# Two decoder layers on one core: the FFN up projection by Strassen's algorithm over pairs of chunks

## The chip, the core and the metric

The kernel runs on one core of a Trainium2 chip, as one program with one launch. The metric is its time on the device in microseconds (us), the median of several executions. The core has five engines that run their own queues in order and wait for each other through semaphores: TensorE (PE in the profile, its weight loads PEld), VectorE (DVE), ScalarE (ACT), GpSimd (POOL) and SyncE (SP), which issues the loads here.

## The reference, cut to what matters

Two layers over 256 tokens of width 1024. Each layer has two half-step FFNs of width 2816, a mixer of three attention branches between them, and a small gated embedding at its end.

```python
def swiglu(x, w1, w3, w2):
    return (jax.nn.silu(x @ w1) * (x @ w3)) @ w2

for i in range(DEPTH):                                   # DEPTH = 2
    h = h + 0.5 * swiglu(rms_norm(h, g_ffn1[i]), w1_a[i], w3_a[i], w2_a[i])
    u = rms_norm(h, g_mix[i])
    h = h + hybrid_mixer(u, ...)
    h = h + 0.5 * swiglu(rms_norm(h, g_ffn2[i]), w1_b[i], w3_b[i], w2_b[i])
    ple_gate = jax.nn.sigmoid(rms_norm(h, g_ple[i]) @ w_ple_gate[i])
    h = h + ple_gate * (p[i] @ w_ple_proj[i])
out = rms_norm(h, g_final)                               # x: (1, 256, 1024) float32
```

All inputs and the output are float32. So there are four FFNs; the change is in their up projections, `x @ w1` and `x @ w3`.

## The kernel before

**Three products for one.** Every float32 operand is split into a high part in a shorter format (`hi`, a ScalarE copy) and the rest (`lo`, a VectorE subtraction); `mm3` (L94 to L97) multiplies hi·hi, hi·lo and lo·hi into one PSUM bank. `load` (L76 to L87) fetches a weight tile of 128x1024 (0.5 MB) into `raw` (4 buffers), and splits it into `whi` and `wlo` (7 buffers each, shared by the whole program).

**An FFN.** The normalized, transposed input lies in `xhi`, `xlo` as 128 rows by 2 token blocks (`tb`) by 8 slices of the model width (`kt`) by 128 tokens; the row factor `r[tb]` of the norm is applied after the product. The width 2816 is cut into 11 chunks of 256 (`NFC`), and a chunk of `w13` holds 256 columns of `w1` and 256 of `w3`, so that one PSUM bank of 512 takes both. `up(c)` multiplies a chunk: 2 token blocks by 8 slices by 3 matmuls of 128x512, 48 in all, from four weight tiles. ScalarE then forms silu of one half (`act`, L203), VectorE the gated product (`pr`, L205). `turn(c)` transposes the product on TensorE and splits it (`fhi`, `flo`); `down` multiplies it by two tiles of `w2`, 24 matmuls, into four banks (`acc`) that gather over all chunks.

**What sets the order.** The loop over chunks writes `up(c)`, then `turn(c-1)`, then `down(c-2)`. A scheduler at build time reorders within the limits of dependences and buffers; at run time each engine takes its list in order, so an instruction that waits holds up all behind it on its engine. The program has eight PSUM banks: two for products (`mm`), two for transposes (`tr`), four for `acc`. GpSimd does the small arithmetic of the norms, on tiles of one column, and three adds of 128x512 in `start_r` (L800) at the program's beginning. `start` loads the input for the first FFN and its first chunk's weights; `soon` and `later` load the constants.

## Time and profile before

| what | value |
|---|---|
| median of 3 runs | 1354.6 us (1354.47 to 1354.67) |
| profiled execution: time, span | 1354.69 us, 1352.9 us |
| granted TensorE clock over the span | 0.997 |
| VectorE's weight splits (L86, 128x1024) | 420 of 1.22 us |
| ScalarE's weight copies (L85, 128x1024) | 420 of 1.05 us |
| weight loads of the four FFNs, 0.5 MB each | 260, 4.3 to 4.5 us from issue to landing |
| loads over the span | 174 GB/s |

How to read the rows below: a row of the timeline has the start in us, the duration (of all its instructions from the first's start to the last's end, where `x` is over 1), the engine, the line, the operation, its output and inputs by the program's names, and in brackets how long the engine had been idle and what ended that. A row of a group has the busy time and the mean of one in ns behind the bar. Durations of matmuls overlap: the distance of two starts is what one costs.

### The profile page before, as it was taken

What the parts mean: (1) busy time and instruction counts of PE and PEld (TensorE: products, weight loads), DVE (VectorE), ACT (ScalarE), POOL (GpSimd) and SP (SyncE); (2) the same over time, 40 slices, a digit from 0 to 9 for tenths busy, and PEclk for the clock granted to TensorE, in tenths of its full rate; (3) what the DMA queues carried; (4) which work ended last, traced back from release to release, by engine and by line L of the source; (5) the groups of instructions that cost most, each with busy time, mean ns of one, the idle gap of its engine ahead of it and who ended that gap; (6) DMA issues with size and microseconds to landing.
All of it is one profiled execution on the core that took longest, in us unless ns stands there. A gap on an engine that the chain in (4) does not pass through costs nothing.

```text
span 1352.9 us, 17897 instructions
## 1 busy us (share of the span) xinstructions
PE 1339.4 (99%) x6720; PEld 1118.3 (83%) x6720; DVE 815.5 (60%) x1190; ACT 731.6 (54%) x1122; POOL 49.3 (4%) x110
## 2 busy tenths in 40 slices
PE   8999999999999999999999999999999999999997
PEld 6888889979788888888888888898788788888886
DVE  6655566666658655555765555665667686655555
ACT  5544456665775544444654444566667745544445
POOL 2000000001000000000100000000010000000000
PEclk9999999999999999999999999999999999999999
DMA  7855547524337565555555555473435465555542
GB/s 261 278 187 190 187 130 223 172 98 152 125 125 218 164 203 187 189 189 190 162 187 187 187 187 187 141 224 126 141 109 160 156 204 173 184 191 187 190 160 83
DMA packets 68343, 236.61 MB, mean 175 GB/s; under 512 B 8225, under 2 KB 8865, under 8 KB 68257
## 3 DMA queue, kind: packets, MB, share of 16 engines
q1 hardware_dynamic: 67824, 234.43, 53.3%
q8 instruction: 52, 0.85, 0.3%
q10 hardware_dynamic: 432, 1.05, 0.2%
q14 instruction: 35, 0.28, 0.1%
HBM read 234.40 MB, written 1.05 MB: 174 GB/s over the span
## 4 chain that ended last, share of the span: by engine, by line
PE 97%; ACT 1%; POOL 1%; DMA 1%; DVE 0%; SPq 0%; issue 0%; POOLq 0%; ACTq 0%
PE mm L95 22%; PE mm L97 21%; PE mm L96 21%; PE acc L95 8%; PE acc L97 8%; PE acc L96 8%; PE tr L216 1%; PE tr L143 1%; PE acc L519 1%; PE tr L512 1%; PE acc L605 1%; PE acc L587 1%; PE tr L475 1%; PE acc L486 1%; DMA xraw<-in_xT 1%; PE acc L543 0%
## 5 line engine op out<-in xcount | busy, mean ns | idle before, releaser
L86 DVE TENSOR_TENSOR wlo<-raw,whi 128x1024 fp32r<-128x1024 f32 (+3 forms) x450 | 535.4, 1201 | 274.7 <-ACT whi L85 255.7
L85 ACT CAST whi<-raw 128x1024 fp32r<-128x1024 f32 (+3 forms) x450 | 456.0, 1028 | 262.0 <-PE acc L97 135.0
L95 PE MATMUL mm<-whi,xhi 128*128 128x512 f32 (+1 forms) x1032 | 404.3, 392 | 1.8 <-ACT whi L85 1.8
L96 PE MATMUL mm<-wlo,xhi 128*128 128x512 f32 (+1 forms) x1032 | 402.1, 390 | 0.6 <-DVE wlo L86 0.6
L97 PE MATMUL mm<-whi,xlo 128*128 128x512 f32 (+1 forms) x1032 | 402.3, 390 | 0.0
L95 PEld LDWEIGHTS mm<-whi,xhi 128*128 128x128 f32 x1032 | 194.0, 188 | 43.2 <-ACT whi L85 2.5
L96 PEld LDWEIGHTS mm<-wlo,xhi 128*128 128x128 f32 x1032 | 194.4, 188 | 40.8 <-DVE wlo L86 2.2
L97 PEld LDWEIGHTS mm<-whi,xlo 128*128 128x128 f32 x1032 | 194.2, 188 | 40.9 <-DVE xlo L129 0.9
L95 PE MATMUL acc<-whi,fhi 128*128 128x512 f32 x352 | 141.0, 402 | 0.0
L203 ACT ACTIVATE act<-mm,r 128x256 f32<-128x256 f32 x88 | 41.8, 475 | 177.2 <-PE mm L97 177.2
L97 PE MATMUL acc<-whi,flo 128*128 128x512 f32 x352 | 137.2, 392 | 0.0
L96 PE MATMUL acc<-wlo,fhi 128*128 128x512 f32 x352 | 136.6, 390 | 0.0
L205 DVE SCALAR_TENSOR_TENSOR pr<-mm,r,act 128x256 f32<-128x256 f32 x88 | 42.3, 481 | 130.9 <-ACT act L203 130.9
L97 PEld LDWEIGHTS acc<-whi,flo 128*128 128x128 f32 x352 | 66.0, 188 | 14.7
L95 PEld LDWEIGHTS acc<-whi,fhi 128*128 128x128 f32 x352 | 66.2, 188 | 13.2 <-ACT fhi L128 1.1
L96 PEld LDWEIGHTS acc<-wlo,fhi 128*128 128x128 f32 x352 | 66.3, 188 | 12.7
L95 PE MATMUL mm<-xhi,whi 128*128 128x256 f32 x256 | 73.9, 288 | 0.0
L97 PE MATMUL mm<-xhi,wlo 128*128 128x256 f32 x256 | 72.4, 283 | 0.0
L96 PE MATMUL mm<-xlo,whi 128*128 128x256 f32 x256 | 72.4, 283 | 0.0
L95 PEld LDWEIGHTS mm<-xhi,whi 128*128 128x128 f32 x256 | 48.9, 191 | 2.0 <-issue 2.0
L96 PEld LDWEIGHTS mm<-xlo,whi 128*128 128x128 f32 x256 | 49.0, 191 | 0.0
L97 PEld LDWEIGHTS mm<-xhi,wlo 128*128 128x128 f32 x256 | 48.9, 191 | 0.0
(213 smaller groups left out, 1361.5 us busy)
## 6 DMA issues: line engine op xcount, KB each, us to landing
raw<-in_w13b SPq DMA_DIRECT2D x88, 512.0 KB, 4.4
raw<-in_w13a SPq DMA_DIRECT2D x84, 512.0 KB, 4.5
raw<-in_wg SPq DMA_DIRECT2D x48, 512.0 KB, 3.8
...
```

The lines of the kernel that those rows point to most:

```text
L85: A.copy(hi[:, c], raw[:, c])
L86: V.tensor_tensor(out=lo[:, c], in0=raw[:, c], in1=hi[:, c].bitcast(F32), op=ALU.subtract)
L95: PE.matmul(o, lhs[0], rhs[0], start=first, stop=False)
L96: PE.matmul(o, lhs[0], rhs[1], start=False, stop=False)
L97: PE.matmul(o, lhs[1], rhs[0], start=False, stop=last)
L143: PE.transpose(t[:, j * P : (j + 1) * P], h[tb][:, k * P : (k + 1) * P], ident)
L203: A.activation(act, o[:, :FC], AF.Silu, scale=r[tb])
L205: V.scalar_tensor_tensor(out=pr, in0=o[:, FC:], scalar=r[tb], in1=act, op0=ALU.mult, op1=ALU.mult)
L216: PE.transpose(t[:, j * S + tb * P : j * S + (tb + 1) * P], prs[tb][:, j * P : (j + 1) * P], ident)
L475: PE.transpose(t[:96, j * P : (j + 1) * P], f[:, 4 * u + j, :], ident)
L486: PE.matmul(o[:, P : 3 * P], q[:, P : 2 * P], k, start=True, stop=True)
L512: PE.transpose(t[:, j * P : (j + 1) * P], e[:, j * P : (j + 1) * P], ident)
```

## The change

Chunks 0 to 9 are taken in five pairs, chunk 10 is multiplied first, as before. For a pair the input (two token blocks by two halves of the model width) and the weights (two halves of the model width by two chunks) are each seen as two by two blocks, and Strassen's algorithm, in Winograd's form, makes the four blocks of the result from 7 products of sums of blocks in place of 8 plain ones.

- `x_forms`, once per FFN, scales the input by the norm's factor (`spread` lays `r` along the free axis) and forms the seven left operands. GpSimd adds `xhi` and `xlo` back together (4 adds of 128x512), VectorE multiplies and adds, and every form is split again. Four of them overwrite `xhi`, `xlo`.
- `w_forms`, once per pair, loads eight tiles (`wr`, 10 buffers; two halves `u` of each of the four blocks). GpSimd forms four differences of 128x1024 for each `u` (`sub`), three of them in place, one in `t2`. ScalarE and VectorE split 14 tiles (`split_w`) in place of 8.
- `pair` runs products 1, 6, 2, 5, 7, 3, 4 (12 matmuls each) into three banks, with the sums of the results in between: `m1` and `m5` are copied out by ScalarE, `u2`, `m5` and `m1` are summed by VectorE, one add by GpSimd. `turn` for the chunks before stands between products, and their `down` after the pair.

A pair has 84 up matmuls in place of 96. The first FFN loads chunk 10 first; the scratch memory of the DMA and two tiles of other stages are made smaller for room.

```diff
+    def split_w(w):
+        hi = wp.tile([P, U], F32R, tag="whi", name=nm("whi"), bufs=7)
+        lo = wp.tile([P, U], F32R, tag="wlo", name=nm("wlo"), bufs=7)
+        A.copy(hi, w)
+        V.tensor_tensor(out=lo, in0=w, in1=hi.bitcast(F32), op=ALU.subtract)
+        return hi, lo
...
+            def gated(c, tb, a, b, scale=None):
+                act = fp.tile([P, FC], F32, tag="act", name=nm("act"))
+                pr = fp.tile([P, FC], F32, tag="pr", name=nm("pr"), bufs=6)
+                if scale is None:
+                    A.activation(act, a, AF.Silu)
+                    V.tensor_tensor(out=pr, in0=b, in1=act, op=ALU.mult)
+                else:
+                    A.activation(act, a, AF.Silu, scale=scale)
+                    V.scalar_tensor_tensor(out=pr, in0=b, scalar=scale, in1=act, op0=ALU.mult, op1=ALU.mult)
+                prs[c, tb] = pr
+
...
+            def quarter(a, at=None):
+                if at is None:
+                    q = [fp.tile([P, 4, P], F32R, tag=f"q{i}", name=nm("q"), bufs=3) for i in range(2)]
+                else:
+                    tb, n = at
+                    q = [x[:, tb, 4 * n : 4 * n + 4, :] for x in (xhi, xlo)]
+                split_T(a.rearrange("p (j t) -> p j t", j=4), *q)
+                return q
+            def x_forms():
+                rbc = fp.tile([P, S], F32, tag="rbc", name=nm("rbc"), bufs=1)
+                spread(r, rbc)
+                a = {}
+                for tb in range(TB):
+                    for n in range(2):
+                        t = a[tb, n] = t512("xn")
+                        t4 = t.rearrange("p (j t) -> p j t", j=4)
+                        c = slice(4 * n, 4 * n + 4)
+                        G.tensor_tensor(
+                            out=t4, in0=xhi[:, tb, c, :].bitcast(F32), in1=xlo[:, tb, c, :].bitcast(F32), op=ALU.add
+                        )
+                        rb = rbc[:, None, tb * P : (tb + 1) * P].to_broadcast([P, 4, P])
+                        V.tensor_tensor(out=t4, in0=t4, in1=rb, op=ALU.mult)
+                s1, s2 = t512("s1"), t512("s2")
+                V.tensor_tensor(out=s1, in0=a[1, 0], in1=a[1, 1], op=ALU.add)
+                V.tensor_tensor(out=s2, in0=s1, in1=a[0, 0], op=ALU.subtract)
+                f = {1: quarter(a[0, 0]), 6: quarter(s2), 2: quarter(a[0, 1]), 5: quarter(s1, (0, 0))}
+                V.tensor_tensor(out=a[1, 0], in0=a[0, 0], in1=a[1, 0], op=ALU.subtract)
+                f[7] = quarter(a[1, 0], (0, 1))
+                V.tensor_tensor(out=s2, in0=a[0, 1], in1=s2, op=ALU.subtract)
+                f[3] = quarter(s2, (1, 0))
+                f[4] = quarter(a[1, 1], (1, 1))
+                return f
+            def w_forms(p):
+                f = {i: [None, None] for i in range(1, 8)}
+                ws = []
+                for u in range(2):
+                    w = {}
+                    for kh, nh in ((0, 0), (0, 1), (1, 1), (1, 0)):
+                        w[kh, nh] = fp.tile([P, U], F32, tag="wr", name=nm("wr"), bufs=10)
+                        nc.sync.dma_start(w[kh, nh], w13[li, 2 * p + nh, 2 * kh + u])
+                    ws.append(w)
+                def sub(out, a, b):
+                    G.tensor_tensor(out=out, in0=a, in1=b, op=ALU.subtract)
+                for u, w in enumerate(ws):
+                    f[1][u] = split_w(w[0, 0])
+                    sub(w[0, 0], w[0, 1], w[0, 0])
+                    t2 = fp.tile([P, U], F32, tag="t2", name=nm("t2"), bufs=2)
+                    sub(t2, w[1, 1], w[0, 0])
+                    f[6][u] = split_w(t2)
+                    f[2][u] = split_w(w[1, 0])
+                    sub(w[0, 1], w[1, 1], w[0, 1])
+                    sub(w[1, 0], w[1, 0], t2)
+                for i, q in ((5, (0, 0)), (7, (0, 1)), (3, (1, 1)), (4, (1, 0))):
+                    for u, w in enumerate(ws):
+                        f[i][u] = split_w(w[q])
+                return f
+            def product(o, x, w, start=False):
+                for kt in range(4):
+                    m = [y[:, (kt % 2) * 512 : (kt % 2) * 512 + 512] for y in w[kt // 2]]
+                    mm3(o, [y[:, kt, :] for y in x], m, start and kt == 0, kt == 3, skip_group_check=True)
+            def pair(p, fx, middle):
+                fw = w_forms(p)
+                oa, ob, oc = bank_mm(), bank_mm(), bank_tr()
+                product(oa, fx[1], fw[1], True)
+                m1 = t512("m1")
+                A.copy(m1, oa)
+                product(ob, fx[6], fw[6], True)
+                u2 = t512("u2")
+                V.tensor_tensor(out=u2, in0=ob, in1=m1, op=ALU.add)
+                product(oa, fx[2], fw[2])
+                gated(2 * p, 0, oa[:, :FC], oa[:, FC:])
+                middle()
+                product(oc, fx[5], fw[5], True)
+                m5 = t512("m5")
+                A.copy(m5, oc)
+                G.tensor_tensor(out=m5, in0=m5, in1=m1, op=ALU.add)
+                product(ob, fx[7], fw[7])
+                V.tensor_tensor(out=m5, in0=ob, in1=m5, op=ALU.add)
+                gated(2 * p + 1, 1, m5[:, :FC], m5[:, FC:])
+                product(oc, fx[3], fw[3])
+                V.tensor_tensor(out=u2, in0=oc, in1=u2, op=ALU.add)
+                gated(2 * p + 1, 0, u2[:, :FC], u2[:, FC:])
+                product(ob, fx[4], fw[4])
+                V.tensor_tensor(out=m1, in0=ob, in1=m1, op=ALU.add)
+                gated(2 * p, 1, m1[:, :FC], m1[:, FC:])
...
-            prs = {}
-            for c in range(NFC):
-                prs[c] = up(c)
-                if first and c == 1:
-                    soon()
-                if first and c == 3:
+                        mm3(acc[2 * tb + n], f, w, c == last and j == 0, c == last - 1 and j == 1)
+
+            up(last)
+            if first:
+                soon()
+            fx = x_forms()
+            acc.extend(bank_acc() for _ in range(4))
+            done = [last]
+            for p in range(NP):
+                def middle(cs=tuple(done)):
+                    for c in cs:
+                        turn(c)
+
+                pair(p, fx, middle)
+                if first and p == 0:
                     later()
-                if c == 5 and aside is not None:
+                if p == 2 and aside is not None:
                     aside()
-                if c == 1:
-                    acc.extend(bank_acc() for _ in range(4))
-                if c >= 1:
-                    turn(c - 1, prs[c - 1])
-                if c >= 2:
-                    un = load2([c - 2])
+                for c in done:
+                    un = load2([c])
                     for tb in range(TB):
                         for n in range(2):
-                            down([c - 2], un, tb, n)
-            turn(NFC - 1, prs[NFC - 1])
-            cs = [NFC - 2, NFC - 1]
-            un = load2(cs)
+                            down([c], un, tb, n)
+                done = [2 * p + 1, 2 * p]
+            for c in done:
+                turn(c)
+            un = load2(done[::-1])
             ro = []
             for tb in range(TB):
                 for n in range(2):
-                    down(cs, un, tb, n)
+                    down(done[::-1], un, tb, n)
...
-            un.append(load(a["w13a"][0, 0, k // 2], step=512))
+            un.append(load(a["w13a"][0, NFC - 1, k // 2], step=512))
```

**VectorE, from the second pair to the third of the first FFN.** In the rows, `wlo<-raw` is a split of a `w2` tile (or, before, of any weight), `wlo<-wr` and `wlo<-t2` a split of a weight form, `pr` a gated product, `flo` a split of transposed products; the numbers behind the names tell buffers apart. Before, a chunk's rows were these:

```order
L86 TENSOR_TENSOR wlo_220_1089<-raw_218_1087,whi_219_1088 128x1024
L129 TENSOR_TENSOR flo_156_767<-tr_190_953,fhi_155_766 128x512
L86 TENSOR_TENSOR wlo_223_1095<-raw_221_1093,whi_222_1094 128x1024
L86 TENSOR_TENSOR wlo_226_1125<-raw_224_1123,whi_225_1124 128x1024
L205 SCALAR_TENSOR_TENSOR pr_213_1049<-mm_211_1022,r_29_203,act_212_1047 128x256
L86 TENSOR_TENSOR wlo_229_1131<-raw_227_1129,whi_228_1130 128x1024
```

Now the end of one pair (`u2`, `m1` of the second) and the beginning of the next are these; the split behind `m1` is that of the next pair's first form:

```order
L327 TENSOR_TENSOR u2_158_666<-tr_156_639,u2_158_666 128x512
L87 TENSOR_TENSOR wlo_185_812<-raw_183_810,whi_184_811 128x1024
L215 TENSOR_TENSOR pr_171_748<-u2_158_666,act_170_747 128x256
L330 TENSOR_TENSOR m1_157_652<-mm_155_638,m1_157_652 128x512
L94 TENSOR_TENSOR wlo_195_857<-wr_186_840,whi_194_856 128x1024
L215 TENSOR_TENSOR pr_173_765<-m1_157_652,act_172_764 128x256
L94 TENSOR_TENSOR wlo_198_864<-t2_196_861,whi_197_863 128x1024
L94 TENSOR_TENSOR wlo_200_868<-wr_189_846,whi_199_867 128x1024
L94 TENSOR_TENSOR wlo_202_874<-wr_190_848,whi_201_873 128x1024
L94 TENSOR_TENSOR wlo_205_881<-t2_203_878,whi_204_880 128x1024
L94 TENSOR_TENSOR wlo_207_885<-wr_193_854,whi_206_884 128x1024
```

The six splits are those of forms 1, 6 and 2 of the first half and then of the second. They go on with forms 5, 7 and 3, and the add of product 6 into `u2` stands behind them:

```order
L94 TENSOR_TENSOR wlo_209_891<-wr_186_840,whi_208_890 128x1024
L94 TENSOR_TENSOR wlo_211_895<-wr_190_848,whi_210_894 128x1024
L94 TENSOR_TENSOR wlo_213_899<-wr_187_842,whi_212_898 128x1024
L94 TENSOR_TENSOR wlo_215_903<-wr_191_850,whi_214_902 128x1024
L94 TENSOR_TENSOR wlo_217_907<-wr_188_844,whi_216_906 128x1024
L315 TENSOR_TENSOR u2_228_951<-mm_225_923,m1_227_937 128x512
```

**GpSimd in the same place.** Before, its list had only the norm's factors here, from the beginning of the first FFN to its end:

```order
L124 TENSOR_TENSOR r_29_203<-ms_28_201,mhalf_80 128x1
L124 TENSOR_TENSOR r_31_207<-ms_30_205,mhalf_80 128x1
L164 TENSOR_SCALAR ss1_321_1566<-ss_318_1561 128x1
L166 TENSOR_SCALAR ms_322_1568<-ss_318_1561,ss1_321_1566 128x1
L168 TENSOR_TENSOR r_323_1570<-ms_322_1568,mhalf_80 128x1
```

Now the add of the second pair and the eight differences of the third stand there:

```order
L322 TENSOR_TENSOR m5_167_714<-m5_167_714,m1_157_652 128x512
L285 TENSOR_TENSOR wr_186_840<-wr_187_842,wr_186_840 128x1024
L285 TENSOR_TENSOR t2_196_861<-wr_188_844,wr_186_840 128x1024
L285 TENSOR_TENSOR wr_187_842<-wr_188_844,wr_187_842 128x1024
L285 TENSOR_TENSOR wr_189_846<-wr_189_846,t2_196_861 128x1024
L285 TENSOR_TENSOR wr_190_848<-wr_191_850,wr_190_848 128x1024
L285 TENSOR_TENSOR t2_203_878<-wr_192_852,wr_190_848 128x1024
L285 TENSOR_TENSOR wr_191_850<-wr_192_852,wr_191_850 128x1024
L285 TENSOR_TENSOR wr_193_854<-wr_193_854,t2_203_878 128x1024
```

The first difference overwrites `wr_186`, which the first split of the pair reads (the fifth row of the second piece).

**TensorE, from product 2 of the second pair on.** `mm_154` is the bank of products 1 and 2, `mm_155` that of 6, 7 and 4, `tr_156` that of 5 and 3:

```order
L105 MATMUL mm_154_637<-whi_136_599,q_50_278 128x512
L103 MATMUL mm_155_638<-whi_142_613,xhi_68 128x512
L104 MATMUL mm_155_638<-wlo_143_614,xhi_68 128x512
L103 MATMUL tr_156_639<-whi_138_605,xhi_68 128x512
L104 MATMUL tr_156_639<-wlo_139_606,xhi_68 128x512
```

The first two matmuls of product 7 were moved ahead of product 5. They write into the bank of product 6, which the first add into `u2` reads.

55 lines of the change are left out of this document (29 added, 26 removed).

## The prediction

> **What bounds the kernel now.** I read the page first (busy time, chain of work that ended last), then the timeline of one stage, then the few places where GpSimd does real work, because that is the engine which the change loads.
>
> ```profile
> PE 1339.4 (99%) x6720; PEld 1118.3 (83%) x6720; DVE 815.5 (60%) x1190; ACT 731.6 (54%) x1122; POOL 49.3 (4%) x110
> ...
> PE 97%; ACT 1%; POOL 1%; DMA 1%; DVE 0%; SPq 0%; issue 0%; POOLq 0%; ACTq 0%
> ```
>
> TensorE is busy for 99% of the span and holds 97% of the chain; GpSimd is nearly empty. So fewer matmuls would pay directly, as long as nothing else becomes late. What a matmul is worth is read from the timeline of an FFN:
>
> ```profile
> 40.13 0.39 PE L97 MATMUL mm<-whi,xlo 128*128 128x512 f32 x1
> ...
> 44.89 0.39 PE L97 MATMUL mm<-whi,xlo 128*128 128x512 f32 x1
> ...
> 45.12 0.60 PE L216 MATMUL tr<-ident,pr 128*128 128x128 f32 x4
> ...
> 45.48 0.48 PE L95 MATMUL acc<-whi,fhi 128*128 128x512 f32 x1
> ```
> ```profile
> 61.74 8.29 SPq L84 DMA_DIRECT2D raw<-in_w13a  x4
> ...
> 145.78 8.29 SPq L84 DMA_DIRECT2D raw<-in_w13a  x4
> ```
>
> Between the first two rows lie 21 matmuls, so one costs (44.89 − 40.13) / 21 = 0.227 us from start to start (its 0.39 us overlap the next). Four transposes take 0.36. The last two rows are the first weight loads of chunks five apart: a chunk lasts 84.04 / 5 = 16.81 us, which is 72 matmuls and the transposes; two chunks 33.6. TensorE has no gap there.
>
> **What goes.** A pair needs 84 up matmuls in place of 96: 12 × 0.227 = 2.7 us, and 20 pairs give 54.4 us. That is all that can be won; TensorE's own work for a pair becomes 132 × 0.227 + 0.8 = 30.7 us.
>
> **What comes, and its prices.** Per pair 8 subtractions of 128x1024 on GpSimd, 14 weight splits (ScalarE copy, VectorE subtract) in place of 8, four VectorE adds of 128x512, one GpSimd add of 128x512. The prices:
>
> ```profile
> L86 DVE TENSOR_TENSOR wlo<-raw,whi 128x1024 fp32r<-128x1024 f32 x420 | 508.7, 1223 | 258.4 <-ACT whi L85 243.7
> ...
> L205 DVE SCALAR_TENSOR_TENSOR pr<-mm,r,act 128x256 f32<-128x256 f32 x88 | 42.3, 481 | 130.9 <-ACT act L203 130.9
> L129 DVE TENSOR_TENSOR flo<-tr,fhi 128x512 fp32r<-128x512 f32 x44 | 30.1, 684 | 0.1
> ```
> ```profile
> 53.17 2.36 DVE L86 TENSOR_TENSOR wlo<-raw,whi 128x1024 fp32r<-128x1024 f32 x2 [0.68 <-ACT whi L85]
> ```
> ```profile
> 17.20 1.28 DVE L86 TENSOR_TENSOR wlo<-raw,whi 128x512 fp32r<-128x512 f32 x2
> ```
> ```profile
> L85 ACT CAST whi<-raw 128x1024 fp32r<-128x1024 f32 x420 | 434.6, 1049 | 255.4 <-PE acc L97 133.4 <-PE mm L97 85.1 <-PE mm L96 25.2
> ```
> ```profile
> L161 POOL TENSOR_TENSOR ss<-ss 128x1 f32<-128x1 f32 x1 | 0.2, 193 | 6.4 <-ACT junk L157 6.4
> ```
>
> A split costs VectorE 1.22 us alone and 2.36 − 1.22 = 1.14 in a row; a 128x512 operation 0.68 and 1.28 − 0.69 = 0.59; a gate product 0.48; a copy costs ScalarE 1.05. GpSimd has three 128x512 adds, and they show more than a price:
>
> ```profile
> 8.93 0.69 DVE L86 TENSOR_TENSOR wlo<-raw,whi 128x512 fp32r<-128x512 f32 x1
> ...
> 9.44 1.34 POOL L800 TENSOR_TENSOR xsq<-xsq,xsq 128x512 f32<-128x512 f32 x1 [8.48 <-ACT xsq L791]
> 9.90 1.43 DVE L86 TENSOR_TENSOR wlo<-raw,whi 128x512 fp32r<-128x512 f32 x1 [0.28 <-ACT whi L85]
> ...
> 13.06 0.69 DVE L793 TENSOR_TENSOR xsq<-xraw 128x512 f32<-128x512 f32 x1
> 13.11 1.80 POOL L800 TENSOR_TENSOR xsq<-xsq,xsq 128x512 f32<-128x512 f32 x1 [2.33 <-ACT xsq L791]
> ...
> 13.66 1.78 DVE L86 TENSOR_TENSOR wlo<-raw,whi 128x512 fp32r<-128x512 f32 x1
> ```
> ```profile
> 14.98 1.62 POOL L800 TENSOR_TENSOR xsq<-xsq,xsq 128x512 f32<-128x512 f32 x1
> 15.37 1.50 DVE L134 SCALAR_TENSOR_TENSOR xlo<-xraw,gcol,xhi 128x256 fp32r<-128x256 f32 x1
> ...
> 16.65 1.05 PE L804 MATMUL acc<-ones,xsq 128*128 128x1 f32 x8 [0.18 <-POOL xsq L800]
> ```
>
> The VectorE split at 9.90 takes 1.43 us instead of 0.69 and ends at 11.33, 0.55 after GpSimd's add (9.44 + 1.34 = 10.78). The second add runs 1.80 us and ends at 14.91, 1.16 after VectorE's operation (13.75); the split from 13.66 ends at 15.44, 0.53 after that add; the third add ends at 16.60, again 1.16 after it; the last row ends at 16.87, 0.27 behind it. So in all these rows **a GpSimd operation and a VectorE operation with two SBUF inputs take turns**, without a gap, each waiting for the other's end; the split, with two SBUF inputs, is the commonest VectorE operation. Its turn takes 0.53 us for 512 columns, so 1.07 for 1024. GpSimd's turn takes 1.16 for 512. For 1024 no row exists: if all of 1.16 grows with the columns it is 2.32; if all of the 0.193 of a one-column add is fixed, 0.193 + 2 × 0.967 = 2.13. I take 2.2, near the middle, since the fixed part is small either way.
>
> The Trainium skill (GPSIMD Engine Reference, section 3.1) gives 4497 ns for a two-input fp32 add of 2048 columns on GpSimd against 2293 on VectorE and advises against elementwise work there. Half of it, an estimate of 2.25 us, would make the whole result some 7 us later than mine.
>
> **One pair in its steady state** (third to fifth of an FFN), from the end of product 4 of the pair before to the end of its own product 4. The order rows say what stands behind what. The first split of the new pair is queued on VectorE behind the add into `m1`, which waits for product 4; every subtraction of the pair waits for that split, because it overwrites the tile.
>
> - The `m1` add 0.69, the first split 1.14 and a gate product of 0.48: 2.3 us.
> - GpSimd then goes through six subtractions (four of the first half, two of the second) before the second `t2`; three splits take turns between them, since form 6 must wait for the first `t2` and the fourth subtraction for the split of `w[1, 0]`: 6 × 2.2 + 3 × 1.07 = 16.4.
> - Two more subtractions, seven splits and the add into `u2` that is queued behind them: 2 × 2.2 + 7 × 1.1 + 0.69 = 12.8. ScalarE's seven copies (7.3) and the `m1` copy run beside.
> - TensorE's first two matmuls of product 7 wait for that add (same PSUM bank), and all of product 5 stands behind them: products 7, 5, 3, 4 are still to come: 48 × 0.227 = 10.9.
>
> Sum 42.4, and ten handovers between engines at about 0.05 (the third add ends at 16.60, its reader starts at 16.65): **42.9 us against 33.6**. Down products, product 1, half of 6 and product 2 lie inside the first three items. TensorE's 30.7 us are no longer the bound; about 12 us of each pair it stands still.
>
> The second pair has its first split and two subtractions ahead of `m1`: 42.9 − 1.1 − 4.4 = about 37. The first pair begins with the up projection of chunk 10. From the last residual add before it to the first `u2` VectorE has 21 operations of 512 columns, 13 splits and 4 small ones (21 × 0.59 + 13 × 1.14 + 1.5 = 28.7), and GpSimd 7 subtractions and 4 adds (20.0), of which I let 17.5 stand in VectorE's way, the others falling beside operations that read PSUM; then 36 matmuls (8.2): 54.4. The tail is two rounds of down products of 10.9 and some 2.0 for transposes and their copies.
>
> An FFN: 54.4 + 37 + 3 × 42.9 + 23.8 = 243.9 us. Before: 11 × 16.81 + 1.1 = 186.0. Four times the difference is 232 us. In the first FFN the last piece of `xT` now stands on SP behind `ident` and `h`, 1.1 MB, some 3 us at the 341 GB/s below. The profiled run took 1354.69 us with a span of 1352.9 (median of the runs 1354.6, the same for this purpose): 1354.7 + 235 = **1590 us**. With the bounds of the subtraction, 37 on the path of each FFN: 148 × (−0.07 or +0.12) = −10 or +18.
>
> **Costed at nothing:** the extra ScalarE copies (18 × 1.05 us and some 4 of smaller work in 43), hidden by VectorE's slower list, and the loads (12 of 0.5 MB per 43 us are 146 GB/s, below the 341 that the windows below show), hidden by two spare buffers. If ScalarE came late, product 2 would wait for the `m1` copy; if a load did, the subtractions would, one for one.
>
> **Rivals.** *The clock.* Gaps now appear in TensorE's work, and the trace has a place for that:
>
> ```profile
> 4.00:8.00 4.00, 2.52 (x13) 1.81 (x13) 2.04 (x4) 2.96 (x7) 0.00 (x0) 1.00 1.01 341
> ...
> 12.00:16.00 4.00, 3.18 (x13) 2.25 (x13) 3.98 (x6) 3.83 (x8) 2.82 (x2) 1.00 0.78 306
> 16.00:20.00 4.00, 3.82 (x18) 2.86 (x17) 3.68 (x6) 0.53 (x1) 1.88 (x3) 0.74 0.66 158
> 20.00:24.00 4.00, 4.00 (x16) 3.24 (x15) 1.93 (x3) 2.47 (x4) 1.08 (x3) 0.83 0.81 300
> 24.00:60.00 36.00, 36.00 (x163) 29.56 (x163) 22.82 (x28) 19.46 (x25) 0.00 (x0) 1.00 0.83 286
> ```
> ```profile
> 18.25 1.05 PE L96 MATMUL mm<-wlo,xhi 128*128 128x512 f32 x2
> 19.11 0.63 PE L97 MATMUL mm<-whi,xlo 128*128 128x512 f32 x1
> ```
>
> After a stretch with gaps the granted clock (last but two) fell to 0.74 and 0.83, and a matmul then cost (19.11 − 18.25) / 2 = 0.43 us. It came back after some 4 us. In a pair the longest gap, some 7 us ahead of the second half of product 6, ends about 9 us before the last 48 matmuls begin, so I count nothing; if 16 of the 48 ran at 0.43, a pair would cost 3.2 more and the kernel 1654; if all, 1785. The Trainium skill (TensorE: Matmul & The Clock Gate, Part 1) halves the clock after an idle window of about 3.4 us; the trace's 0.43 against 0.227 fits, and the long gap would trigger it.
>
> *No turns at this size.* If the two engines ran side by side, the same queue gives 1.9 + two subtractions, copy and split of form 6 (6.7), a split, subtractions four to six (7.7 in all), copy, seven splits, `u2` (9.8), then 10.9 and 0.5: about 38, an FFN 210, the kernel 1450. All five of the ends above speak against it.
>
> *The other side: faster.* If the splits and subtractions of a pair ran ahead during the products of the pair before, TensorE would be the bound: 54 us won, less some 4 us of forms of `x` per FFN: 1316. GpSimd's 4% and the empty 40% of VectorE speak for it, the place of the first split behind `m1` against it. It decides when the four items above fall from 42.9 below 33.6.
>
> **How the numbers follow.** My forecast 0.74, its own range 1530 to 1650; the clock 0.12; no turns 0.08; faster 0.05; no change 0.01. The low end 1500 leaves room for GpSimd and VectorE overlapping in part, the high end 1680 takes in the milder clock case; the two ends of the subtraction lie inside. Faster by over 0.2% (about what a measurement of this kernel can tell from no change) 0.05, within 0.01, slower 0.94.
>
> **What would show it.** Subtractions of 128x1024 at about 2.2 us or, beside splits, 3.3; splits that show up to 3.3 us where they wait for GpSimd; VectorE far busier by its rows while TensorE falls to some 75 to 80%; a pair every 43 us, with the longest TensorE gap ahead of the second half of product 6 and another ahead of product 7. The prediction is wrong if the subtractions start before product 4 ends, if splits stay at 1.22 beside them, or if GpSimd needs much more or less than 2.2 us.

## The result, and the profile after

The changed kernel takes 1660.9 us (median of 4 runs, 1659.3 to 1664.7) against 1354.5 before: 1.227 times as long, with a 95% interval of 1.225 to 1.229. The profiled execution took 1660.5 us, with a span of 1658.7. The forecast was 1590 with a range of 1500 to 1680: the sign and the place were right, and 71 us were missing. The time lies 11 us above the stretch that the forecast gave to its own mechanism (1530 to 1650); the range went further up to leave room for the lowered clock.

The page of the changed kernel, its first part (busy time and share of the span), and from its groups by line and shape those of the differences, of the splits beside them, and of the multiplications of the input (`xn`) by the norm's factor:

```profile
PE 1393.5 (84%) x6496; PEld 1121.0 (68%) x6496; DVE 1158.0 (70%) x1458; ACT 874.2 (53%) x1314; POOL 527.8 (32%) x306
```
```profile
L285 POOL TENSOR_TENSOR wr<-wr,wr 128x1024 f32<-128x1024 f32 x80 | 194.1, 2426 | 134.4 <-DVE wlo L94 85.0 <-DMA raw<-in_w2a 32.9 <-DMA raw<-in_w2b 16.4
L285 POOL TENSOR_TENSOR wr<-wr,t 128x1024 f32<-128x1024 f32 x40 | 134.2, 3354 | 124.5 <-issue 70.5 <-DVE wlo L94 43.5 <-ACT xhi L136 10.5
L285 POOL TENSOR_TENSOR t<-wr,wr 128x1024 f32<-128x1024 f32 x40 | 95.9, 2397 | 3.0
L94 DVE TENSOR_TENSOR wlo<-t,whi 128x1024 fp32r<-128x1024 f32 x40 | 88.5, 2213 | 226.6 <-ACT whi L93 226.6
L261 DVE TENSOR_TENSOR xn<-xn,rbc 128x512 f32<-128x512 f32 x16 | 33.4, 2148 | 1.5 <-ACT rbc L193 1.5
```

TensorE fell from 99% of the span to 84% (forecast 75 to 80). It has 224 instructions fewer and is busy for longer than before (1393.5 us against 1339.4), since part of them ran at a lowered clock, as below. A difference takes 2.40 us where nothing holds it (`t`), 3.35 in the fourth place of a half. The splits of `t` take 2.21 in place of 1.22, and VectorE stood idle for 226.6 us ahead of them, because their ScalarE copy waited for GpSimd. So in 36 of the 40 halves VectorE first waits for GpSimd and is then held by it; the exceptions are the second halves of each FFN's first pair (1.21 to 1.22, with no wait). The split isn't the only operation that is held: the multiplications of the input take 2.15, and 0.68 in the run below that has no differences. The page's chain of work breaks off after 3% of the span in this kernel and can't be used.

One steady pair, from one add into `m1` to the next: the timelines of VectorE and of GpSimd (start, duration, engine, line, operation, idle time before it and what ended that).

```profile
686.94 0.68 DVE L330 TENSOR_TENSOR m<-mm,m 128x512 f32<-128x512 f32 x1
687.54 1.21 DVE L94 TENSOR_TENSOR wlo<-wr,whi 128x1024 fp32r<-128x1024 f32 x1
...
694.93 2.33 DVE L94 TENSOR_TENSOR wlo<-t,whi 128x1024 fp32r<-128x1024 f32 x1 [5.84 <-ACT whi L93]
697.18 2.35 DVE L94 TENSOR_TENSOR wlo<-wr,whi 128x1024 fp32r<-128x1024 f32 x2
707.61 2.29 DVE L94 TENSOR_TENSOR wlo<-t,whi 128x1024 fp32r<-128x1024 f32 x1 [8.08 <-ACT whi L93]
709.83 9.05 DVE L94 TENSOR_TENSOR wlo<-wr,whi 128x1024 fp32r<-128x1024 f32 x6
718.80 0.68 DVE L315 TENSOR_TENSOR u<-mm,m 128x512 f32<-128x512 f32 x1
...
730.14 1.21 DVE L87 TENSOR_TENSOR wlo<-raw,whi 128x1024 fp32r<-128x1024 f32 x1
731.28 0.41 DVE L215 TENSOR_TENSOR pr<-u,act 128x256 f32<-128x256 f32 x1
731.61 0.68 DVE L330 TENSOR_TENSOR m<-mm,m 128x512 f32<-128x512 f32 x1
```
```profile
688.89 2.45 POOL L285 TENSOR_TENSOR wr<-wr,wr 128x1024 f32<-128x1024 f32 x1 [8.22 <-DVE wlo L94]
...
693.77 2.40 POOL L285 TENSOR_TENSOR wr<-wr,wr 128x1024 f32<-128x1024 f32 x1
698.53 3.25 POOL L285 TENSOR_TENSOR wr<-wr,t 128x1024 f32<-128x1024 f32 x1 [2.35 <-issue]
701.73 2.35 POOL L285 TENSOR_TENSOR wr<-wr,wr 128x1024 f32<-128x1024 f32 x1
...
706.46 2.36 POOL L285 TENSOR_TENSOR wr<-wr,wr 128x1024 f32<-128x1024 f32 x1
```

The turns are seen at two places. The split at 694.93 ends at 697.26, which is 1.09 after GpSimd's difference (693.77 + 2.40 = 696.17): it waited for the end and then took its own time. The difference at 698.53 ends at 701.78, 2.25 after the second of two splits (697.18 + 2.35 = 699.53). The pair lasts 731.61 − 686.94 = 44.67 us, and its four steps are: `m1` add and first split until GpSimd begins, 1.95; six differences and their turns until 706.46, 17.57; the rest up to the end of the `u2` add (718.80 + 0.68), 13.02; from there to the next `m1` add 12.13.

TensorE in the same pair: the three longest gaps in its timeline, and four of the six stretches into which the pair was cut (us, then busy time and count for PE, PEld, DVE, ACT, POOL, then the granted clock, DMA share, GB/s).

```profile
707.63 0.80 PE L103 MATMUL mm<-whi,q 128*128 128x512 f32 x1 [5.26 <-ACT whi L93]
709.96 0.80 PE L104 MATMUL mm<-wlo,q 128*128 128x512 f32 x1 [1.53 <-DVE wlo L94]
719.53 0.50 PE L103 MATMUL mm<-whi,xhi 128*128 128x512 f32 x1 [1.91 <-DVE u L315]
```
```profile
698.00:706.00 8.00, 3.44 (x14) 2.17 (x12) 1.53 (x2) 0.00 (x0) 7.40 (x3) 0.94 0.00 0
706.00:711.00 5.00, 1.84 (x4) 1.14 (x5) 3.39 (x3) 4.47 (x5) 2.82 (x2) 0.50 0.00 0
711.00:718.80 7.80, 6.62 (x24) 4.97 (x22) 7.80 (x6) 6.02 (x9) 3.22 (x1) 0.73 0.49 149
718.80:724.00 5.20, 4.46 (x19) 3.52 (x20) 4.93 (x7) 2.06 (x4) 0.15 (x1) 1.00 0.97 369
```

The long gap stands ahead of the second half of product 6 and the other ahead of product 7, where the prediction had put them. Behind the first the granted clock is 0.50, then 0.73; it is back at 1.00 when product 7 begins.

### The profile page after: what moved, and what is told of

Its sections match the earlier page's. It is cut to its first block, busy times and chain, and to the rows that moved or that the text cites. A ratio compares the mean times of both kernels' runs of the same rounds, so it can differ in the third digit from the quotient of the medians.

```text
span 1658.7 us, 18342 instructions
## 1 busy us (share of the span) xinstructions
PE 1393.5 (84%) x6496; PEld 1121.0 (68%) x6496; DVE 1158.0 (70%) x1458; ACT 874.2 (53%) x1314; POOL 527.8 (32%) x306
## 5 line engine op out<-in xcount | busy, mean ns | idle before, releaser
L87 DVE TENSOR_TENSOR wlo<-raw,whi 128x1024 fp32r<-128x1024 f32 (+3 forms) x290 | 347.9, 1208 | 109.5 <-ACT whi L86 106.7
L86 ACT CAST whi<-raw 128x1024 fp32r<-128x1024 f32 (+3 forms) x290 | 288.2, 1015 | 126.5 <-PE mm L105 31.6
L94 DVE TENSOR_TENSOR wlo<-wr,whi 128x1024 fp32r<-128x1024 f32 x240 | 328.0, 1412 | 10.0 <-ACT whi L93 10.0
L93 ACT CAST whi<-wr 128x1024 fp32r<-128x1024 f32 x240 | 242.8, 1046 | 105.0 <-issue 48.0
L103 PE MATMUL mm<-whi,xhi 128*128 128x512 f32 (+1 forms) x552 | 222.3, 403 | 40.2 <-DVE u L315 37.0
L94 DVE TENSOR_TENSOR wlo<-t,whi 128x1024 fp32r<-128x1024 f32 x40 | 88.5, 2213 | 226.6 <-ACT whi L93 226.6
L285 POOL TENSOR_TENSOR wr<-wr,wr 128x1024 f32<-128x1024 f32 x80 | 194.1, 2426 | 134.4 <-DVE wlo L94 85.0
L105 PE MATMUL mm<-whi,xlo 128*128 128x512 f32 (+1 forms) x552 | 218.1, 395 | 5.0 <-DVE xlo L137 3.9
L104 PE MATMUL mm<-wlo,xhi 128*128 128x512 f32 (+1 forms) x552 | 217.3, 394 | 0.0
L103 PE MATMUL mm<-whi,q 128*128 128x512 f32 x240 | 118.1, 492 | 108.2 <-ACT whi L93 88.0
L285 POOL TENSOR_TENSOR wr<-wr,t 128x1024 f32<-128x1024 f32 x40 | 134.2, 3354 | 124.5 <-issue 70.5
L103 PE MATMUL acc<-whi,fhi 128*128 128x512 f32 x352 | 138.0, 396 | 17.5 <-ACT whi L86 10.6
L105 PE MATMUL mm<-whi,q 128*128 128x512 f32 x240 | 109.3, 455 | 12.8 <-DVE q L137 12.7
```

The source lines that it names most:

```text
L86: A.copy(hi[:, c], raw[:, c])
L87: V.tensor_tensor(out=lo[:, c], in0=raw[:, c], in1=hi[:, c].bitcast(F32), op=ALU.subtract)
L93: A.copy(hi, w)
L94: V.tensor_tensor(out=lo, in0=w, in1=hi.bitcast(F32), op=ALU.subtract)
L103: PE.matmul(o, lhs[0], rhs[0], start=first, stop=False, **more)
L104: PE.matmul(o, lhs[0], rhs[1], start=False, stop=False, **more)
```

## The experiments

Three theories were held against each other. **A**: the pair is as long as the lists of VectorE and GpSimd make it, with their turns and with the `u2` add queued behind the splits. **B**: the lowered clock of TensorE makes it. **Q**, for the later runs: the two engines run side by side, or their turns fill only time in which the pair waits for GpSimd anyway. Distances between the adds into `m1` are called a pair, as above; all are of the second FFN, steady pairs. Ratios are to the kernel before, with 95% intervals.

### The differences moved, and left out

Differences on VectorE:

```diff
-                    G.tensor_tensor(out=out, in0=a, in1=b, op=ALU.subtract)
+                    V.tensor_tensor(out=out, in0=a, in1=b, op=ALU.subtract)
```

> The eight differences of weights of each pair are formed on VectorE instead of GpSimd; all else stays. Theory A (a pair is set by the list of splits and differences on VectorE and GpSimd, which take turns, and by what is queued behind them): a difference then costs 1.14 us in a row instead of 2.35 and its turns vanish; VectorE has 26 operations of 1.14 and some 6 us of others per pair, 36 in all, so a steady pair falls from 44.7 to 36 to 38 us and the kernel from 1661 to 1500 to 1540 us, still slower than 1354.6. Theory B (the lowered clock of TensorE makes most of the loss beyond the removed matmuls): the gaps become shorter but stay, a pair stays above 41 us and the kernel above 1590.

1575.9 us, ratio 1.164 [1.160, 1.167]; pairs of 40.1, 40.0 and 41.8. That is between the two forecasts. TensorE's longest gap and two stretches say why:

```profile
681.19 0.77 PE L103 MATMUL mm<-whi,xhi 128*128 128x512 f32 x1 [7.23 <-DVE u L315]
```
```profile
673.00:681.00 8.00, 0.96 (x9) 0.72 (x7) 8.00 (x9) 4.77 (x7) 0.00 (x0) 0.83 0.82 264
681.00:685.50 4.50, 4.31 (x11) 3.34 (x12) 1.57 (x4) 0.18 (x1) 0.00 (x0) 0.55 0.57 231
```

`u2` still waits behind the splits, VectorE being busy for all of the 8 us ahead of it. Here the gap ends just where product 7 begins, so the clock is low (0.55) for the first 11 matmuls behind it, and they take 4.5 us in place of 2.5. So B is not idle talk: it costs some 2 us a pair here, but only because of where this gap ends.

No differences; the forms are plain blocks:

```diff
-                    G.tensor_tensor(out=out, in0=a, in1=b, op=ALU.subtract)
+                    pass
...
-                    f[6][u] = split_w(t2)
+                    f[6][u] = split_w(w[1, 1])
```

> The differences of weights are left out altogether: forms 6, 5, 7, 3 and 4 are splits of plain blocks, so the FFNs are not those of the reference; 14 splits, 7 products and all sums of results stay. Theory A: VectorE has 18 splits of 1.14 and some 6 us of others per pair, 26 us, below TensorE's 30.7, so TensorE is the bound again; a steady pair takes 31 to 34 us and the kernel 1315 to 1360. If the 14 splits or the order of the sums of results were the cause and not GpSimd's work, a pair would stay above 38 us and the kernel above 1450.

1357.4 us, ratio 1.002 [1.001, 1.004]; pairs of 30.9, which is about the 30.7 of TensorE's own work. So the differences carry nearly all of the 306 us, whatever their mechanism. Even for nothing they leave no gain: 54 us of matmuls are saved and spent again. The next run asks where. It takes out the forms of the input as well, and with them the norm's factor:

```diff
-                    A.activation(act, a, AF.Silu)
+                    A.activation(act, a, AF.Silu, scale=1e-3)
...
-                rbc = fp.tile([P, S], F32, tag="rbc", name=nm("rbc"), bufs=1)
-                spread(r, rbc)
...
+                qs = [[x[:, tb, 4 * n : 4 * n + 4, :] for x in (xhi, xlo)] for tb in range(TB) for n in range(2)]
+                return {i: qs[i % 4] for i in range(1, 8)}
```

> As the run without differences, and the forms of the input left out too (the seven left operands are plain blocks of the input, without the norm's factor, and the gate's input is scaled by a constant); the output is not the reference's. Theory A (in that run the start of each FFN, where the forms are made, eats the saving): kernel 1296 to 1320, and the first pair of an FFN, 41 us there, 30 to 33. Rival (the saving is lost elsewhere, in the later pairs or the tail): above 1340, first pair 38 or more.

1324.7 us, ratio 0.978 [0.974, 0.982], 5 us above Theory A's stretch; the first pair, from the last residual add ahead of the FFN to its `m1` add, fell from 41.1 to 32.3 us. So the forms of the input cost 33 us a kernel, some 8 per FFN. Of the 54 us of matmuls 30 then show as a gain (1354 to 1324.7); the other 24 were not followed further.

### The clock

28 matmuls without use stand between the two halves of product 6, so that the long gap is filled:

```diff
+                def fill():
+                    d = bank_tr()
+                    rhs = fx[1][0].rearrange("p j t -> p (j t)")
+                    for i in range(28):
+                        PE.matmul(d, fx[1][0][:, i % 4, :], rhs, start=i == 0, stop=i == 27)
...
-                product(ob, fx[6], fw[6], True)
+                product(ob, fx[6], fw[6], True, fill)
```

> 28 matmuls of 128x512 on the forms of x, into a spare bank that nobody reads, stand between the two halves of product 6, where a steady pair's longest gap of TensorE lies (28 x 0.227 = 6.4 us); what is computed stays the same. Theory A: the granted clock in the stretch behind the gap rises from 0.5 to 0.73 to about 1, but the second half of product 6 waits for its split as before, so a steady pair stays at 44.7 within 0.5 us; the kernel changes by less than 1.5%, more likely upwards, by the fill in the first pairs of each FFN. Theory B: with the full clock a pair falls by 2 us or more and the kernel by 40 us or more.

1686.4 us, ratio 1.245 [1.242, 1.249], 25 us longer than without the filling. Two stretches of one of its pairs, and in it the splits ahead of `u2` and the beginning of product 5:

```profile
718.00:724.00 6.00, 6.00 (x27) 4.65 (x25) 4.00 (x3) 5.08 (x6) 3.65 (x3) 1.00 0.00 1
724.00:730.20 6.20, 3.94 (x21) 3.10 (x20) 6.20 (x5) 5.05 (x8) 2.85 (x1) 1.00 0.40 124
```
```profile
722.26 7.95 DVE L94 TENSOR_TENSOR wlo<-wr,whi 128x1024 fp32r<-128x1024 f32 x5
```
```profile
735.20 0.50 PE L103 MATMUL tr<-whi,xhi 128*128 128x512 f32 x1 [1.53 <-DVE flo L137]
```

From 718 on, products 6 and 2 run at the full clock, where the changed kernel has 0.50 and 0.73, and `u2` comes 30.9 us behind `m1` in place of 31.9. But here five splits stand in the row ahead of `u2`, in the changed kernel six (709.83 above), and in both VectorE goes from them to the `u2` add without a pause: the 1 us is the one split less, and these rows show no gain from the clock. The pair got longer all the same (46.4, where A expected 44.7 within 0.5), because its second part grew from 12.8 to 15.5 us. Product 5 waits for a split of the transposed products (the last row), which stands behind three splits of weight forms here and straight behind `u2` in the changed kernel. So the filling changed the scheduler's order too, and only the part up to `u2` can be compared. B falls as the main cause.

### Who waits for whom

The splits of four forms written behind the `u2` add, first with the differences on GpSimd, then with them on VectorE:

```diff
-                for i, q in ((5, (0, 0)), (7, (0, 1)), (3, (1, 1)), (4, (1, 0))):
-                    for u, w in enumerate(ws):
-                        f[i][u] = split_w(w[q])
-                return f
+                def rest(*qs):
+                    for i, q in qs:
+                        for u, w in enumerate(ws):
+                            f[i][u] = split_w(w[q])
+                return f, rest
...
                 V.tensor_tensor(out=u2, in0=ob, in1=m1, op=ALU.add)
+                rest((5, (0, 0)), (7, (0, 1)), (3, (1, 1)), (4, (1, 0)))
```

> The splits of forms 5, 7, 3 and 4 are written behind the add of product 6 into u2, so that this add no longer stands behind them in VectorE's list; the same work otherwise. Theory A (lists of VectorE and GpSimd, with turns, and the add queued behind the splits): about 4 to 6 us of each pair's 44.7 go, to 39 to 41 (the turns themselves, eight differences and the splits between them, stay as a floor of some 39), kernel 1555 to 1590. Rival Q (the add's place in the queue doesn't matter, since all the splits are needed by the end of the pair anyhow): within 1% of 1661, pair 44 to 45.

> Both edits: the add into u2 ahead of the splits of forms 5, 7, 3 and 4, and all differences on VectorE. Theory A: VectorE's own list is then the bound, eight differences of about 1.2, eighteen splits of 1.14 and some 5 us of small operations, 35 to 36 us a pair; kernel 1480 to 1530, still above 1354.5. Rival Q: the early add gains nothing over differences on VectorE alone, 1560 to 1580.

With GpSimd 1662.6 us, ratio 1.227 [1.224, 1.231]: nothing is gained, and what A expected there is refuted. The first pairs are shorter (53.0 for 59.1 in the second FFN), the steady ones longer (46.7 to 49.5, where A expected 39 to 41). In one of them `u2` comes 27.6 us behind `m1` in place of 31.9, but the next `m1` add 19.3 us behind `u2` in place of 12.8. TensorE's timeline names what is late next:

```profile
725.29 0.76 PE L103 MATMUL tr<-whi,xhi 128*128 128x512 f32 x1 [1.29 <-DVE flo L137]
```

Product 5 (the row), which writes into a bank of the transposes' pool, now waits for the split of the transposed products, and that stands behind five splits of weight forms on VectorE. With the differences on VectorE the same edit gives 1465.2 us, ratio 1.082 [1.078, 1.085], 15 us below the expected stretch, and the pair is what its list takes (35.3 us, VectorE busy for 34.9 of them, the clock at 1.00):

```profile
613.12:648.43 35.31, 33.02 (x142) 25.42 (x141) 34.91 (x38) 21.07 (x26) 5.00 (x1) 1.00 0.45 150
```

These two kernels differ in their source only in the engine of the differences: 197 us, or 11.6 in a pair (46.9 against 35.3). Of these 6.3 lie ahead of `u2` (27.6 against 21.3) and 5.3 behind it, where the scheduler laid out the rest differently: with the differences on VectorE product 5 doesn't wait for the split of transposed products behind the weight splits. So the 197 us are not the engine's alone. The next kernel shares the load, with the first two differences of each half on VectorE and two on GpSimd:

```diff
-                def sub(out, a, b):
-                    G.tensor_tensor(out=out, in0=a, in1=b, op=ALU.subtract)
+                def sub(out, a, b, eng):
+                    eng.tensor_tensor(out=out, in0=a, in1=b, op=ALU.subtract)
...
+                E = V
...
-                    sub(w[0, 0], w[0, 1], w[0, 0])
+                    sub(w[0, 0], w[0, 1], w[0, 0], E)
...
-                    sub(t2, w[1, 1], w[0, 0])
+                    sub(t2, w[1, 1], w[0, 0], E)
...
-                    sub(w[0, 1], w[1, 1], w[0, 1])
-                    sub(w[1, 0], w[1, 0], t2)
+                    sub(w[0, 1], w[1, 1], w[0, 1], G)
+                    sub(w[1, 0], w[1, 0], t2, G)
```

> The early add into u2, and the first two differences of each half (the one over the first block, and t2) on VectorE, the other two on GpSimd. Theory A (a GpSimd difference and a VectorE operation take turns, so what GpSimd takes over costs VectorE's lane 2.3 us in place of the 1.2 that it would need itself): slower than with all eight on VectorE, pair 37 to 42 us, kernel 1490 to 1590. Rival Q (the two engines work side by side, and a load shared between them is done sooner): pair 31 to 35 us, kernel 1370 to 1460, faster than with all eight on VectorE.

1592.2 us, ratio 1.176 [1.173, 1.179]: 127 us slower than with all on VectorE (2 us above what A expected, its pairs of 43.2 to 46.3 above too). VectorE and GpSimd at one place of a pair, the whole pair, and the beginning of product 5 in it:

```profile
662.37 3.42 DVE L285 TENSOR_TENSOR t<-wr,wr 128x1024 f32<-128x1024 f32 x1
```
```profile
662.25 2.46 POOL L285 TENSOR_TENSOR wr<-wr,wr 128x1024 f32<-128x1024 f32 x1 [7.32 <-DMA raw<-in_w2b]
```
```profile
660.30:703.65 43.35, 35.28 (x141) 27.18 (x140) 36.94 (x33) 21.24 (x26) 13.73 (x5) 0.92 0.37 121
```
```profile
691.86 0.77 PE L103 MATMUL tr<-whi,xhi 128*128 128x512 f32 x1 [0.71 <-DVE flo L137]
```

VectorE's own difference, 1.22 us alone, lasts 3.42, ending 1.08 after GpSimd's (664.71), which began 0.12 ahead of it. Over the pair VectorE is busy for 36.94 us, though four operations left its list, in place of 34.91: what GpSimd takes over costs VectorE's lane more than it saves, as A had it, and the two engines did not do the load sooner side by side.

That is some 2 us of the 8 by which this pair is longer (43.4 against 35.3). The rest lies in the order: `u2` comes 20.7 us behind `m1` (21.3 with all on VectorE), but the next `m1` add 22.7 behind `u2` in place of 14.0, since product 5 waits again for a split of transposed products, behind seven splits of weight forms. So the 127 us are not the price of sharing alone.

### What the turns are worth

First three fills in place of each difference (two of 1024 columns and one of 512), which read nothing:

```diff
-                    G.tensor_tensor(out=out, in0=a, in1=b, op=ALU.subtract)
+                    G.memset(out, 0.01)
+                    G.memset(out, 0.02)
+                    G.memset(out[:, :512], 0.03)
```

> Each difference on GpSimd is replaced by three memsets of the same tile (1024, 1024 and 512 columns, by the one memset of the program, 0.2 us for 128 columns, about 2.4 us together), so GpSimd is as busy as before in the same places but reads nothing; the weight forms are constants and the FFNs not those of the reference. Theory A, with the turns due to both engines reading their operands: splits beside GpSimd cost 1.2 us again and a steady pair falls from 44.7 to 38 to 40, the kernel to 1540 to 1580. If a GpSimd operation of any kind holds VectorE off, pair and kernel stay within 2% of 44.7 and 1661, splits still reach 3 us. If turns were no cost at all, likewise no change, but with splits of 1.2 us on both.

1385.7 us, ratio 1.023 [1.020, 1.026], far below the expectation, with splits of 1.24 to 1.30 us. The run tells less than it was meant to: a fill has no input, so the fills of `t` run ahead of their place, and their splits no longer wait for the chain. It shows only that fills don't hold VectorE and that GpSimd's time alone, out of the chain, costs little (28 us over the kernel without differences). So the chain was put back, by a two-input operation on one column ahead of the fills (the third difference reads `t2`, to keep the order):

```diff
-                    G.tensor_tensor(out=out, in0=a, in1=b, op=ALU.subtract)
+                    G.tensor_tensor(out=out[:, 0:1], in0=a[:, 0:1], in1=b[:, U - 1 : U], op=ALU.subtract)
+                    G.memset(out, 0.01)
+                    G.memset(out, 0.02)
+                    G.memset(out[:, :512], 0.03)
...
-                    sub(w[0, 1], w[1, 1], w[0, 1])
+                    sub(w[0, 1], w[0, 1], t2)
```

> Each difference becomes a two-input operation on one column and three fills of the same tile behind it, about 2.4 us of GpSimd's time as before and kept in the same order by dependences (the third waits for t2 instead of its own second input); the fills read nothing, and the output is not the reference's. The first split now stands ahead of the last add into m1 and u2 behind three more splits, which about cancel. Theory A (the turns have a price of their own): splits at 1.2 to 1.3 us, a half's four differences from the first to the next half's first in 9.6 to 11 us in place of 12.84, pair 38 to 41 us, kernel 1540 to 1605. Rival Q (the turns only fill time in which the pair waits for GpSimd anyway): the half still takes 12.5 to 13, pair 43.5 to 45, kernel above 1630.

1586.9 us, ratio 1.172 [1.168, 1.176], pairs of 42.1 to 43.2: the time lies in A's stretch, the pairs between the theories, and the stand-in took 2.76 us from start to start, not 2.4. The first split stands ahead of the `m1` add here, so that GpSimd begins 0.22 us behind the start of that add in place of 1.95:

```profile
655.76 0.68 DVE L333 TENSOR_TENSOR m<-mm,m 128x512 f32<-128x512 f32 x1
```
```profile
655.98 0.19 POOL L285 TENSOR_TENSOR wr<-wr,wr 128x1 f32<-128x1 f32 x1 [10.45 <-DVE wlo L94]
```

So this run can't be compared with the changed kernel step by step. With the last fill cut to 128 columns:

```diff
-                    G.memset(out[:, :512], 0.03)
+                    G.memset(out[:, :128], 0.03)
```

> As the run with fills kept in order, the last fill cut from 512 to 128 columns, so that a difference's stand-in takes GpSimd 2.35 to 2.45 us from start to start, as a real difference does, in place of the 2.76 measured there. Theory A (the turns have a price of their own): a half's four stand-ins in 10.3 to 11.2 us in place of the real ones' 12.84, splits at 1.2 to 1.3, pair 38.5 to 41, kernel 1510 to 1560, so that about 100 to 150 of the 306 us added are the turns. Rival Q (the turns only fill time in which the pair waits for GpSimd anyway): half 12.5 to 13, pair 43.5 to 45, kernel above 1620.

1618.4 us, ratio 1.195 [1.190, 1.200], pairs of 43.0 to 44.6. The stand-in now takes 2.44 (674.80 to 677.24 for `t`), and the first split stands behind the `m1` add again, as in the changed kernel. GpSimd, the splits ahead of `u2` on VectorE, TensorE and two stretches:

```profile
672.29 0.25 POOL L285 TENSOR_TENSOR wr<-wr,wr 128x1 f32<-128x1 f32 x1 [8.22 <-DVE wlo L94]
...
680.83 1.10 POOL L285 TENSOR_TENSOR wr<-wr,t 128x1 f32<-128x1 f32 x1 [1.11 <-DVE wlo L94]
...
683.93 0.19 POOL L285 TENSOR_TENSOR wr<-wr,wr 128x1 f32<-128x1 f32 x1
```
```profile
691.10 9.17 DVE L94 TENSOR_TENSOR wlo<-wr,whi 128x1024 fp32r<-128x1024 f32 x8
```
```profile
701.02 0.77 PE L103 MATMUL mm<-whi,xhi 128*128 128x512 f32 x1 [5.80 <-DVE u L318]
```
```profile
692.00:700.20 8.20, 3.21 (x8) 1.97 (x6) 8.20 (x9) 6.74 (x9) 3.21 (x4) 0.71 0.66 223
700.20:705.00 4.80, 3.98 (x9) 2.98 (x10) 2.20 (x5) 0.07 (x1) 0.00 (x0) 0.50 0.69 274
```

A half takes 683.93 − 672.29 = 11.64 us in place of 12.84 (701.73 − 688.89): the turns have a price, but a small one, 1.2 us a half, since the fourth operation must wait for a split that comes late even without them. (One turn is left: the one-column add at 680.83 takes 1.10 in place of 0.19, beside a split.) The first half of the pair is shorter, `u2` 29.8 us behind `m1` with two more splits ahead of it; but the gap ahead of `u2` now ends at product 7, the clock is 0.50 there, and the next `m1` add comes 14.8 us behind `u2` in place of 12.8. Without the turns the kernel is 43 us shorter; A expected 100 to 150 and Q under 41. That understates the turns. The two more splits ahead of `u2` are 2.3 us of VectorE's time, so with the old order `u2` would stand some 27.6 us behind `m1` in place of 31.9: an estimate of 4.3 us a pair, 86 for the twenty, for the turns up to `u2`. No run has it without the two splits and with the clock kept up, so the price of the turns stays between 43 us, measured, and some 86, estimated, out of the 306. What costs most is the chain through GpSimd itself: nearly the same fills took 1385.7 us where the splits did not wait for them, and 1618.4 where they did.

The last two runs ask which operations take turns: one input in place of two on GpSimd, then on VectorE.

```diff
-                    G.tensor_tensor(out=out, in0=a, in1=b, op=ALU.subtract)
+                    G.tensor_scalar(out=out, in0=a if out is b else b, scalar1=0.5, scalar2=None, op0=ALU.mult)
```

> Each difference becomes a product with 0.5 of the one input that keeps the order between them; all places, buffers and lists stay, GpSimd reads one tile in place of two, so the output is not the reference's. Theory A, if a GpSimd operation with one SBUF input takes turns with a split as well: splits beside it still show over 1.8 us, and the pair shortens only by what eight operations are shorter, to 38 to 42 us, kernel 1550 to 1630. Theory A, if only two inputs on GpSimd take turns: splits stay near 1.22 and the pair falls to 33 to 37, kernel 1400 to 1480. Rival Q (no turns at all, the pair is long since GpSimd is slow and the dependences make VectorE wait): splits near 1.22 in any case, and the pair follows GpSimd's own time alone.

```diff
-        V.tensor_tensor(out=lo, in0=w, in1=hi.bitcast(F32), op=ALU.subtract)
+        V.tensor_scalar(out=lo, in0=w, scalar1=hi.bitcast(F32)[:, 0:1], scalar2=None, op0=ALU.subtract)
```

> The split's second VectorE input becomes one column of the copy (a scalar for each row): VectorE reads one SBUF tile in place of two, each wait stays, the differences stay on GpSimd as they are; the output is not the reference's. Theory A (two-input operations of VectorE take turns with GpSimd's): the splits beside differences fall to 1.2 or below, the differences to about 2.35 everywhere, and the pair to about 38 us, kernel 1430 to 1490 (what the prediction gave the case without turns, 1450). Rival Q (GpSimd's slowness and the dependences alone): splits at most 0.1 to 0.2 shorter, pair 43 to 45, kernel above 1620. If one-input operations take turns as well, it is also above 1600, with splits beside differences above 1.8.

The first gave 1629.0 us, ratio 1.202 [1.199, 1.206], pairs of 43.2; the second 1555.2 us, ratio 1.148 [1.142, 1.154], pairs of 39.5 to 40.9. GpSimd and VectorE of the first, then of the second:

```profile
685.57 2.77 POOL L285 TENSOR_SCALAR wr<-wr 128x1024 f32<-128x1024 f32 x1
689.23 3.62 POOL L285 TENSOR_SCALAR wr<-t 128x1024 f32<-128x1024 f32 x1 [0.88 <-POOL wr L285]
```
```profile
686.72 1.23 DVE L94 TENSOR_TENSOR wlo<-t,whi 128x1024 fp32r<-128x1024 f32 x1 [6.60 <-ACT whi L93]
```
```profile
650.71 2.41 POOL L285 TENSOR_TENSOR wr<-wr,wr 128x1024 f32<-128x1024 f32 x1
```
```profile
644.95 0.75 DVE L94 TENSOR_SCALAR wlo<-wr,whi 128x1024 fp32r<-128x1024 f32 x1
...
651.88 1.80 DVE L94 TENSOR_SCALAR wlo<-t,whi 128x1024 fp32r<-128x1024 f32 x1 [5.84 <-ACT whi L93]
```

In the first, a split beside GpSimd's one-input operation keeps its 1.23 us: it is not held. But that operation takes 2.77 (2.78 is the mean of the 40 for `t`, with no split beside them), more than the two-input one. The other way round GpSimd still waits: its operation at 689.23 began while a split ran until 690.21, and lasted 3.62. A half takes 12.89 us as against 12.84, so what the held splits had cost went into GpSimd's longer chain; the pair follows that chain, as Q had it, though Q's "no turns at all" is not borne out. In the second, the one-input split (0.75 alone) lasts 1.80 beside a difference and ends at 653.68, 0.56 after it (650.71 + 2.41 = 653.12): it is held as the two-input one was. So the case in which one-input operations take turns as well is the true one; its figure, above 1600, was wrong because I forgot that the splits themselves would be shorter, 0.75 in place of 1.22.

The Trainium skill (SBUF — State Buffer, section "SBUF: two separate sides") tells of a port pair that VectorE and GpSimd hold one at a time for a whole instruction, and names two-input operations of VectorE and one-input ones in a two-port mode. The turns here agree; the 1.80 of the one-input split agrees too, if it ran in such a mode, which no row names (it took 0.75 alone, the two-input one 1.22). It has them held against any GpSimd operation that reads SBUF; the 1.23 beside GpSimd's one-input operation differs, and here the measurement decides.

## Why the prediction was right in sign and short in size

**The place and the sign: shown.** Differences left out: 1357 us; nearly the same GpSimd time, out of the chain: 1386. So the differences and the wait for them are the cause; the prediction's chain through VectorE, GpSimd and the `u2` add was the right one to add up.

**The steps of the steady pair**, forecast against measured: `m1` add and first split 2.3, 1.95 (the gate product runs beside GpSimd's first difference). Six differences and three turns 16.4, 17.57. Two differences, seven splits and `u2` 12.8, 13.02. The 48 matmuls 10.9 with 0.5 of handovers, 12.13. Sum 42.9, 44.67.

- **The price of a difference was the step that was mis-sized in the steady pair.** I took 2.2 us between 2.13 and 2.32. The six of this step take 7.28 (688.89 to 696.17), 2.25 (from the split's end) and 4.68 us (701.78 to 706.46), 2.37 each and so above my upper bound; only the one that had waited lies inside. That is 1.0 us of the 1.17 by which the second item is longer. The estimate of 2.25 from the Trainium skill (GPSIMD Engine Reference, section 3.1) was nearer but below the rows too.
- **The turn of a split** was right: 1.09 us, forecast 1.07.
- **The end of the pair was forecast too short.** Product 4's last matmul ends at 730.85 (the row below), yet the `m1` add starts at 731.61: a split of `w2` and a gate product stand ahead of it on VectorE (730.14 and 731.28 above). That queue was left out, 0.76 us a pair.

```profile
730.46 0.39 PE L105 MATMUL mm<-whi,xlo 128*128 128x512 f32 x1
```

**The other parts of an FFN** (the second one, from the last residual add ahead of it to its own last, 260.0 us against the forecast 243.9): first pair 59.1 for 54.4, second 40.4 for 37, three steady ones 134.2 for 128.7, tail 26.3 for 23.8. So of the 16.1 us that are missing, the three steady pairs hold 5.5 and the other parts 10.6: the larger part of the miss stands where the sum was coarser. Four FFNs give 304 us more than before, forecast 235. In the first pair 1.9 us are missing up to `u2` (48.1 for 46.2) and 2.7 behind it (10.9 for 8.2): there TensorE had stood still for 4.22 us, and the granted clock over the next 11 us is 0.78. Some 2 of these 2.7 us are the clock (the first ten matmuls behind the gap take 4.3 us in place of 2.3), the rest is the `u2` add itself (0.68). The clock I had counted as nothing everywhere: right for the steady pair, wrong here. That the time still fell into the range owes something to luck: the room up to 1680 was left for the clock, and other terms filled most of it.

```profile
591.68 0.80 PE L103 MATMUL mm<-whi,xhi 128*128 128x512 f32 x1 [4.22 <-DVE u L315]
```
```profile
591.00:602.00 11.00, 10.32 (x37) 8.36 (x38) 8.85 (x13) 2.83 (x4) 2.85 (x2) 0.78 0.64 240
```

In the tail one wait of TensorE, 1.74 us for a ScalarE copy of transposed products, makes most of the 2.5 us. The second pair and the tail were not tested by runs of their own.

**The rivals.** *The clock* (1654 us): its total came close by accident, its mechanism did not act where I put it. The rule of the Trainium skill (TensorE: Matmul & The Clock Gate, Part 1) agrees with the 0.50 after the gaps; filling the gap of the steady pair gained nothing that the rows show. *No turns* (1450): refuted in its price. The turns exist, and with them nearly gone the kernel still took 1618, since the chain of eight serial operations on GpSimd stays. *Faster* (1316): it needed the differences to run ahead; even without any the kernel takes 1357.

**No version here beats the kernel before.** The best with the whole computation is 1465 us. Its steady pairs take 35.3 us, bounded by VectorE's list of 34.9, against 33.6 for two chunks before. These twelve pairs make 20 of the 111 us by which it is longer; the rest, in the first two pairs and the tails, was not followed.
